# Low halves of split weights written one block later, splitting spread between matmul groups, and shared tiles in the hybrid attention units

## The chip, the cores and the metric

The kernel runs on one core of one Trainium2 chip. The metric is the device time of one execution in microseconds (us). The median of three runs is 2098.37 us. A core has TensorE (PE, with PEld for its weight loads), VectorE (DVE), ScalarE (ACT), GpSimd (POOL) and SyncE (SP, which here issues the loads of the weights). Each engine works through its own list of instructions in order and waits at semaphores for the others.

## The reference, cut to what matters

256 tokens of width 1024 pass two blocks of (feed-forward, attention, feed-forward), then a block with a hybrid attention (8 heads over a block of the sequence, 8 heads over the 64 keys that an indexer's top-k selects) and a mixture that picks experts by top-16 searches (PEER). All is float32.

```python
for i in range(2):
    kv = mem_n @ mem_w_kv[i]
    x = x + 0.5 * swiglu(rmsnorm(x, norm_g[i, 0]), ffn_w_up[i, 0], ffn_w_down[i, 0])
    h = rmsnorm(x, norm_g[i, 1])
    mix = pool_layer(h, ...) if i == 0 else diff_layer(h, ...)   # in-projection, attention, out-projection
    x = x + mix
    x = x + 0.5 * swiglu(rmsnorm(x, norm_g[i, 2]), ffn_w_up[i, 1], ffn_w_down[i, 1])
x = rmsnorm(x, final_norm_g)
mod = silu(c) @ w_ada + b_ada                                    # six rows: shifts, scales, gates
h = modulate(rms_norm(x, norm_attn), sh1, sc1)
x = x + g1 * hybrid_mixer(h, w_in, w_out, rel_bias)
h = modulate(rms_norm(x, norm_ffn), sh2, sc2)
x = x + g2 * peer_ffn(h, peer_wq, peer_subkeys, peer_u, peer_v)
return rms_norm(x, norm_final)
```

In the hybrid mixer each chunk of 128 queries does `score = einsum(wi, relu(qi @ k_idx))`, `top_k(score, 64)`, and a softmax over the selected keys; the other eight heads do a causal softmax with a position bias.

## The kernel before

Every float32 product is made of three matmuls. A factor is split into a high part that TensorE takes as it is and a low part, the rest: a block of weights `raw` [128 x 1024] is loaded by SP, ScalarE copies it to `whi` (L144), VectorE subtracts to `wlo` (L145), and `mm3` (L184 to L186) does high x high, the two mixed products, and no more. Activations are split the same way into `hT_hi` and `hT_lo` (L192 to L201).

The weights form one stream, `items`, in the order of use. `split_one` handles the next item of the stream: it emits `whi` and `wlo` (or, for an item with a `call`, a piece of the modulation row, two VectorE steps `acc` in `ada_piece`, L463 and L465). `nextw` gives out the next block and first splits as many blocks as `cfg["ahead"]` says, four, beyond it; `fetch(4)` asks for four blocks, enough for a projection of 512 columns. So when a group of matmuls is fetched, the splits of the next four blocks are written in one piece into the lists of ScalarE and VectorE. `load_to` issues the loads five blocks ahead.

`proj_cols` makes a projection in four quanta of 24 matmuls (8 blocks of 128 rows, three products each); a block of weights holds two of the eight, so the fourth block is first used by the 19th matmul and its low part by the 21st. Each quantum ends with `yield`, and the attention code interleaves it with steps of the softmax: the order of every engine's list is the order in which the Python code calls. After two quanta `evac` takes the result out; in the feed-forward layer (`ffn`) that is `silu` (L520 to L522) and `gate` (L532). `rows_mm` does the same with 12 matmuls of 512 columns, `out_proj_k` the out-projections, in which the last segments (`tail`) run row by row, with `update` (L1030, L1031), `stats` and `realT` (`ma`, `xg`, `hT_hi`; L343 to L355) of the next norm between them.

In the differential layer a unit's steps on VectorE are `e` (scores with bias, L850), `mx`, `nb`, the reciprocal `rc` and scalings (L866 to L872), `pt` (transposed probabilities, L884), `ov` (L911), then `cat_hi` and `cat_lo` (L198, L201), the operand of the out-projection.

The hybrid attention has eight units (`make(t, g)`: token half t, four heads g) of four steps: `s0` scores, bias, maximum and exponentials (one tile `e` for two heads, L1124 to L1142); `s1` reciprocals and four scalings on VectorE (L1148, L1152); `s2` eight or four transposes and the copy `pt` (L1164); `s3` the product with the values and the split of `yA` or `yB`. `pipeline` runs s1 of one unit, a quantum of the projections (`fill`), s0 of a later one, s3 and s2. `select` (L1090, L1091) runs ahead of all that: eight rounds of MAX and MATCH_REPLACE for each token half.

Of the kernel before, what the change touches and what calls it, by code (L numbers as in the profile page):

```python
# [60 lines left out]
def kernel(ctx: ExitStack, tc: tile.TileContext, A, LAY, stop=None):  # L61
# [41 lines left out]
    st = {"load": 0, "split": 0, "use": 0, "nsplit": 0, "raw": {}, "s": {}}  # L103
    deferred = []
    cfg = {"raw": 5, "ahead": 4}
# [288 lines left out]
    def out_proj_k(segs, update, nxt, tail=2, ahead=None):  # L394
# [12 lines left out]
        for gi in range(n - tail):  # L407
            gots[gi] = [fetch(1), fetch(1)]
            for t in range(NT):
                for h in range(2):  # L410
                    mm(t, h, [gi], gots)
                if t:
                    run_deferred()
                yield
# [5 lines left out]
        for t in range(NT):  # L420
            for h in range(2):
# [16 lines left out]
                if cut < n:  # L438
                    ahead.append(fetch(4))
                    cfg.update(was)  # L440
                yield
# [310 lines left out]
    n2 = Norm(A["norm_g"][0, 2])  # L752
    with pool("pl") as sp:
# [8 lines left out]
        def u_part(h):  # L762
            got = fetch(4)
            for t in range(NT):
                n1.before(t)
                p = pmm()
                rows_mm(p, hT, got[:4], t, 0, 512, 8)
                yield
                rows_mm(p, hT, got[4:], t, 0, 512, 8)
                ACT.activation(u[t][:, h * 512:(h + 1) * 512], p, AF.Copy, scale=n1.rstd[:, t:t + 1])  # L770
                if t:
                    run_deferred()
                yield
# [10 lines left out]
        def mixed():  # L784
# [4 lines left out]
            for ct in range(8):  # L789
# [6 lines left out]
                if ct % 2:  # L796
                    yield
# [8 lines left out]
        drain(fill)  # L806
    kv0.close()
# [13 lines left out]
    n5 = Norm(A["norm_g"][1, 2])  # L821
    with pool("df") as sp:
# [99 lines left out]
        def v_part(h):  # L922

            got = fetch(4)
            for t in range(NT):
                n4.before(t)
                p = pmm()
                rows_mm(p, hT, got[:4], t, 0, 512, 8)
                yield
                rows_mm(p, hT, got[4:], t, 0, 512, 8)  # L930
                ACT.activation(v[:, t, h * 512:(h + 1) * 512], p, AF.Copy, scale=n4.rstd[:, t:t + 1])
                if t:
                    run_deferred()
                yield
# [17 lines left out]
        drain(o)  # L952
    kv1.close()
# [49 lines left out]

    gotv, got = m1.got
# [95 lines left out]
    def v_part():  # L1100
        got = fetch(4)
        for t in range(NT):
            p = pmm()
            rows_mm(p, hT, got[:4], t, 0, 512, 8)
            yield
            rows_mm(p, hT, got[4:], t, 0, 512, 8)
            ACT.activation(av[:, t, 512:], p, AF.Copy)
            if t:
                run_deferred()
            yield  # L1110

    def make(t, g):

        w = (t + 1) * P
        b = {}

        def s0():
            pj = []
            for j in range(2):
                p = psm().rearrange("p (i s) -> p i s", i=2)  # L1120
                r = slice(j * 64, (j + 1) * 64)
                for i in range(2):
                    ct = 2 * g + i
                    PE.matmul(p[:, i, :w], aq[r, ct, t * P:(t + 1) * P], ak[r, ct, :w], start=True, stop=True)  # L1124
                pj.append(p)
            b["e"], b["s"] = [], []
            for j in range(2):
                bias = strip[:, 4 * g + j:4 * g + j + 3:2, S - w:]
                e = sp.tile([P, 2, S], F32, name="e", tag="e", bufs=6)
                V.scalar_tensor_tensor(e[:, :, :w], pj[j][:, :, :w], 0.125, bias, op0=OP.mult, op1=OP.add)  # L1130
                b["e"].append(e)
            if g >= 2:
                for j in range(2):
                    e = b["e"][j][:, :, :w]
                    V.tensor_tensor(e, e, M[:, t, None, :w].to_broadcast([P, 2, w]), op=OP.add)
            for j in range(2):
                e = b["e"][j]
                mx, nb, sm = (small([P, 2], x, bufs=6) for x in ("mx", "nb", "sum"))
                V.tensor_reduce(mx, e[:, :, :w], axis=AX.X, op=OP.max)
                V.tensor_scalar(nb, mx, -1.0, None, op0=OP.mult)  # L1140
                for i in range(2):
                    ACT.activation(e[:, i, :w], e[:, i, :w], AF.Exp, bias=nb[:, i:i + 1], accum_out=sm[:, i:i + 1])  # L1142
                b["s"].append(sm)

        def s1():
            rcs = [small([P, 2], "rc", bufs=6) for _ in range(2)]
            for j in range(2):
                V.reciprocal(rcs[j], b["s"][j])  # L1148
            for j in range(2):
                for i in range(2):  # L1150
                    e = b["e"][j][:, i, :w]
                    V.tensor_scalar(e, e, rcs[j][:, i:i + 1], None, op0=OP.mult)  # L1152

        def s2():
            n = 2 * (t + 1)
            b["p"] = []
            for j in range(2):
                p = ptr()
                for i in range(2):
                    for m in range(t + 1):  # L1160
                        c = i * (t + 1) + m
                        tr(p[:, c * P:(c + 1) * P], b["e"][j][:, i, m * P:(m + 1) * P])
                pt = sp.tile([P, 4, P], F32, name="pt", tag="pt", bufs=4)
                V.tensor_copy(pt[:, :n, :], p[:, :n * P].rearrange("p (m t) -> p m t", t=P))  # L1164
                b["p"].append(pt)

        def s3():
            p = psm()
            for i in range(2):
                for j in range(2):  # L1170
                    h = 4 * g + 2 * i + j
                    for m in range(t + 1):
                        PE.matmul(p[j * 64:(j + 1) * 64, i * P:(i + 1) * P], av[:, m, h * 64:(h + 1) * 64],
                                  b["p"][j][:, i * (t + 1) + m, :], start=m == 0, stop=m == t)
# [6 lines left out]
    for i, _ in enumerate(itertools.chain(proj_cols(hT, 4, 4, col_evac(aq, 0)), proj_cols(hT, 4, 4, col_evac(ak, 0)))):  # L1181
# [5 lines left out]
        else:  # L1187
            step(*se)
    drain(*se)
# [6 lines left out]
    for n, _ in zip(counts, pipeline(units, [(1, 2), (None, 0), (3, 3), (2, 2), (0, 0)])):  # L1196
        for _ in range(n):
            step(fill)
    drain(fill)
# [3 lines left out]

    got = m2.got
# [91 lines left out]
    q1st.close()  # L1296
    wstack.close()
# [337 lines left out]
```

## Time and profile before

| | before |
|---|---|
| median of 3 runs | 2098.37 us (2098.26 to 2100.83) |
| the profiled execution | 2098.71 us, its span 2096.9 us |
| mean granted clock of TensorE | 0.987 |
| TensorE busy | 2033.5 us (97%), 13678 matmuls |
| VectorE busy | 1458.4 us (70%) |
| ScalarE busy | 985.5 us (47%) |
| moved by DMA | 416.93 MB, 199 GB/s in the mean |

The stages in the profile: key and value projections of the memory until 62 us, feed-forward 62 to 255, pool layer to 350, feed-forward to 545 and to 735, differential layer to 893, feed-forward to 1086, hybrid attention to 1246, the query projection and top-16 to 1320, then the routing and the experts to 2097. A granted clock of 1.00 is 2.4 GHz; the other level is 1.2 GHz, and a window's figure is the mean over it.

### The profile page before, as it was taken

The page shows a single profiled execution, that of the slowest core. Times are in us where ns is not written, and L with a number is a line of the kernel's source. Part 1 is how long each engine was busy: PE and PEld are TensorE (multiplying, and loading weights), DVE is VectorE, ACT ScalarE, POOL GpSimd, SP SyncE. Part 2 cuts the span into 40 slices and gives each one's busy share as a digit, 9 for nine tenths or more (in the row PEclk, how much of TensorE's full clock was granted, in tenths as well). Part 3 has the DMA queues.
Part 4 walks back from the last instruction along what each step waited for, and adds up shares of the span by engine and source line. Part 5 has one row for each costly group of instructions (what it writes and reads, how often), then busy time and mean ns, then how long its engine had stood idle before and what let it go on. Part 6 is the DMA issues. An engine that isn't in the chain of part 4 may idle for free. (4 is left out here: it accounts for less than half of the span.)

```text
span 2096.9 us, 34488 instructions
## 1 busy us (share of the span) xinstructions
PE 2033.5 (97%) x13678; PEld 1832.0 (87%) x13678; DVE 1458.4 (70%) x2330; ACT 985.5 (47%) x1508; POOL 39.0 (2%) x74
## 2 busy tenths in 40 slices
PE   8999999999999998899989899999999999999998
PEld 7999888998999797799878779999998888888886
DVE  6677566776677568756658688889976666666666
ACT  6444454444444445354444344455554444444444
POOL 2000000000000000000000000000000000000000
PEclk9999999999999999999999899999999999999999
DMA  7667535676576552355545333556676776777764
GB/s 274 217 236 266 188 134 205 227 250 233 185 248 244 187 195 101 120 191 198 206 124 180 104 98 134 175 178 213 245 252 209 226 231 207 225 243 225 225 211 140
DMA packets 142379, 416.93 MB, mean 199 GB/s; under 512 B 12469, under 2 KB 47429, under 8 KB 140041
## 3 DMA queue, kind: packets, MB, share of 16 engines
q1 hardware_dynamic: 102672, 372.04, 52.4%
q10 hardware_dynamic: 37976, 36.91, 5.5%
q0 software_dynamic: 1568, 5.77, 0.9%
q8 instruction: 107, 1.75, 0.3%
q14 instruction: 56, 0.45, 0.1%
HBM read 396.82 MB, written 17.86 MB: 198 GB/s over the span
## 5 line engine op out<-in xcount | busy, mean ns | idle before, releaser
L145 DVE TENSOR_TENSOR wlo<-raw,whi 128x1024 fp32r<-128x1024 f32 (+1 forms) x654 | 780.6, 1222 | 329.8 <-ACT whi L144 329.5
L144 ACT ACTIVATE whi<-raw 128x1024 fp32r<-128x1024 f32 (+1 forms) x654 | 663.0, 1048 | 147.6 <-PE mm L186 85.4
L184 PE MATMUL mm<-hT_hi,whi 128*128 128x256 f32 x1680 | 479.9, 286 | 0.0
L185 PE MATMUL mm<-hT_lo,whi 128*128 128x256 f32 x1680 | 473.1, 282 | 0.0
L186 PE MATMUL mm<-hT_hi,wlo 128*128 128x256 f32 x1680 | 472.9, 281 | 0.0
L184 PEld LDWEIGHTS mm<-hT_hi,whi 128*128 128x128 f32 x1680 | 319.0, 190 | 6.5 <-issue 6.1
L185 PEld LDWEIGHTS mm<-hT_lo,whi 128*128 128x128 f32 x1680 | 318.9, 190 | 2.0 <-issue 1.9
L186 PEld LDWEIGHTS mm<-hT_hi,wlo 128*128 128x128 f32 x1680 | 318.7, 190 | 0.0
L184 PE MATMUL sm<-hT_hi,whi 128*128 128x256 f32 (+1 forms) x1048 | 299.5, 286 | 5.4 <-DVE hT_hi L192 2.2
L186 PE MATMUL sm<-hT_hi,wlo 128*128 128x256 f32 (+1 forms) x1048 | 296.5, 283 | 4.4 <-DVE wlo L145 4.4
L185 PE MATMUL sm<-hT_lo,whi 128*128 128x256 f32 (+1 forms) x1048 | 296.1, 283 | 0.4 <-DVE hT_lo L195 0.4
L184 PEld LDWEIGHTS sm<-hT_hi,whi 128*128 128x128 f32 (+1 forms) x1048 | 199.2, 190 | 8.7 <-DVE hT_hi L192 2.6
L184 PE MATMUL mm<-whi,wh 128*128 128x512 f32 x512 | 204.1, 399 | 2.1 <-ACT wh L194 2.1
L186 PEld LDWEIGHTS sm<-hT_hi,wlo 128*128 128x128 f32 (+1 forms) x1048 | 199.2, 190 | 4.8 <-DVE wlo L145 4.8
L186 PE MATMUL mm<-whi,wl 128*128 128x512 f32 x512 | 202.2, 395 | 0.0
L185 PEld LDWEIGHTS sm<-hT_lo,whi 128*128 128x128 f32 (+1 forms) x1048 | 199.3, 190 | 2.8 <-DVE hT_lo L195 0.6
L185 PE MATMUL mm<-wlo,wh 128*128 128x512 f32 x512 | 201.5, 394 | 0.0
L194 ACT ACTIVATE wh<-wf 128x256 fp32r<-128x256 f32 x128 | 53.5, 418 | 215.6 <-DVE wf L1484 215.6
L184 PE MATMUL mm<-whi,gT_hi 128*128 128x512 f32 x352 | 140.0, 398 | 0.0
L186 PE MATMUL mm<-whi,gT_lo 128*128 128x512 f32 x352 | 139.5, 396 | 0.0
L185 PE MATMUL mm<-wlo,gT_hi 128*128 128x512 f32 x352 | 138.6, 394 | 0.0
L1316 ACT ACTIVATE act<-sm 128x256 f32<-128x256 f32 x128 | 49.1, 384 | 166.3 <-PE sm L186 166.3
(308 smaller groups left out, 2615.9 us busy)
## 6 DMA issues: line engine op xcount, KB each, us to landing
raw<-in_ffn_up_dram SPq DMA_DIRECT2D x176, 512.0 KB, 5.2
raw<-in_peer_u_dram SPq DMA_DIRECT2D x128, 512.0 KB, 3.7
raw<-in_peer_v_dram SPq DMA_DIRECT2D x128, 512.0 KB, 3.8
raw<-in_ffn_dn_dram SPq DMA_DIRECT2D x88, 512.0 KB, 5.2
raw<-in_w_ada_dram SPq DMA_DIRECT2D x48, 512.0 KB, 5.0
gall<-stage ACTq DMA_DIRECT2D x16, 1024.0 KB, 4.6
G<-gall ACTq DMA_DIRECT2D x16, 1024.0 KB, 7.2
raw<-in_diff_w_in_dram SPq DMA_DIRECT2D x28, 512.0 KB, 5.5
```

The costliest lines, as they stand in the source:

```text
L144: ACT.activation(hi[:, :n], r[:, :n], AF.Copy)
L145: V.tensor_tensor(lo[:, :n], r[:, :n], hi[:, :n].bitcast(F32), op=OP.subtract)
L184: PE.matmul(out, a[0], b[0], start=start, stop=False)
L185: PE.matmul(out, a[0], b[1], start=False, stop=False)
L186: PE.matmul(out, a[1], b[0], start=False, stop=stop)
L194: ACT.activation(hi, src, AF.Copy)
L1316: ACT.activation(act[n], p, AF.Gelu)
```

## The change

The low half of a block is no longer emitted with its high half: `split_one` puts it on a list (`st["low"]`), and `low_one` emits it when a second one is pending, when the item is a `call`, or when `nextw` gives the block out. In the pool, differential and hybrid layers `cfg["spread"]` is set: `nextw` splits nothing ahead, and `ahead_one`, called after each quantum, splits one block if fewer than four are ahead. In the hybrid units the four heads of the first token half share one tile `e` and one maximum, the maximum is negated in its own instruction, one reciprocal serves four heads, and two of the four scalings are ScalarE's. The later steps of the second half's selection run between the steps of the first units.

```diff
+    def low_one():
+
+        j, r, p_ = st["low"].pop(0)
+        c = st["s"][j]
+        nk, w = items[j][1:3]
+        lo = p_.tile([P, CH], F32R, name="wlo", tag="wlo", bufs=4)
+        V.tensor_tensor(lo[:, :nk * w], r[:, :nk * w], c.hi.rearrange("p k w -> p (k w)").bitcast(F32), op=OP.subtract)
+        c.lo = lo[:, :nk * w].rearrange("p (k w) -> p k w", w=w)
+
     def split_one():
+
         j = st["split"]
-        load_to(j + cfg["raw"])
+        load_to(j + cfg["raw"] - len(st["low"]))
...
             hi = p_.tile([P, CH], F32R, name="whi", tag="whi", bufs=4)
-            lo = p_.tile([P, CH], F32R, name="wlo", tag="wlo", bufs=4)
             ACT.activation(hi[:, :n], r[:, :n], AF.Copy)
-            V.tensor_tensor(lo[:, :n], r[:, :n], hi[:, :n].bitcast(F32), op=OP.subtract)
-            st["s"][j] = Split(hi[:, :n].rearrange("p (k w) -> p k w", w=w), lo[:, :n].rearrange("p (k w) -> p k w", w=w))
+            st["s"][j] = Split(hi[:, :n].rearrange("p (k w) -> p k w", w=w), None)
+            st["low"].append((j, r, p_))
         st["split"] += 1
-        load_to(j + 1 + cfg["raw"])
+        while len(st["low"]) > 1 or st["low"] and call is not None:
+            low_one()
+        load_to(j + 1 + cfg["raw"] - len(st["low"]))
...
-        while k < len(items) and ahead < cfg["ahead"]:
+        while k < len(items) and ahead < cfg["ahead"] and not cfg["spread"]:
             ahead += items[k][3] is None
             k += 1
         while st["split"] < k:
             split_one()
+        while st["s"][j].lo is None:
+            low_one()
...
+    def ahead_one():
+
+        if cfg["spread"] and st["split"] < min(st["use"] + 4, len(items)):
+            split_one()
...
                 if j:
+                    ahead_one()
                     yield
                 proj_col(act, got, c0 + j, p[:, j * S:(j + 1) * S])
             evac(c0, m, p[:, :m * S].rearrange("p (j t) -> p j t", t=S))
+            ahead_one()
             yield
...
+            mx, sm = (small([P, 4], x, bufs=6) for x in ("mx4", "sum4"))
...
+            for k, e in enumerate(b["e"]):
+                c = k * heads
+                V.tensor_reduce(mx[:, c:c + heads], e, axis=AX.X, op=OP.max, negate=True)
+                for i in range(heads):
+                    ACT.activation(e[:, i], e[:, i], AF.Exp, bias=mx[:, c + i:c + i + 1], accum_out=sm[:, c + i:c + i + 1])
 
         def s1():
...
+            rc = small([P, 4], "rc4", bufs=6)
+            V.reciprocal(rc, b["s"])
+            for c in range(4):
+                e = b["e"][c // heads][:, c % heads]
+                if c < 2:
+                    V.tensor_scalar(e, e, rc[:, c:c + 1], None, op0=OP.mult)
+                else:
+                    ACT.activation(e, e, AF.Copy, scale=rc[:, c:c + 1])
...
-            step(*se)
-    drain(*se)
+            step(*(se if i == 1 else se[1:] if i == 7 else se[:1]))
...
+        if 1 <= i <= 4:
+            step(se[1])
+        elif i == 5:
+            drain(*se)
     drain(fill)
...
+    cfg["spread"] = False
     got = m2.got
```

TensorE's list is the same before and after, names aside; VectorE's and ScalarE's lists move. Three places follow. In the changed kernel L137 is `wlo`, L153 `whi`.

VectorE in the differential layer, where a unit's heads are put into `cat`, before:

```order
L872 SCALAR_TENSOR_TENSOR e<-e,rc 128x128 x2
L249 TENSOR_SCALAR ms<-oss 128x4
L145 TENSOR_TENSOR wlo<-raw,whi 128x1024 x4
L198 TENSOR_SCALAR cat_hi<-tr,sng 128x4x128
L201 SCALAR_TENSOR_TENSOR cat_lo<-tr,sng,cat_hi 128x4x128
```

and with the change:

```order
L901 SCALAR_TENSOR_TENSOR e<-e,rc 128x128 x2
L269 TENSOR_SCALAR ms<-oss 128x4
L137 TENSOR_TENSOR wlo<-raw,whi 128x1024 x2
L216 TENSOR_SCALAR cat_hi<-tr,sng 128x4x128
L219 SCALAR_TENSOR_TENSOR cat_lo<-tr,sng,cat_hi 128x4x128
```

Two of the four `wlo` have moved ahead, between the steps of the units before; the rest of the order is the same.

VectorE where the hybrid layer's out-projection ends and the modulated norm of the next part begins (`ma`, `xg`, `hT_hi`), before:

```order
L145 TENSOR_TENSOR wlo<-raw,whi 128x1024 x4
L1030 TENSOR_TENSOR xg<-mm,grow 128x512
L1031 TENSOR_TENSOR x_65<-x_65,xg 128x512
L192 CAST hT_hi<-sm 128x2x128
L195 TENSOR_TENSOR hT_lo<-sm,hT_hi 128x2x128
L1030 TENSOR_TENSOR xg<-mm,grow 128x512
L1031 TENSOR_TENSOR x_65<-x_65,xg 128x512
L320 SCALAR_TENSOR_TENSOR s_12355<-ssm 128x1
L337 TENSOR_SCALAR hh_12326<-x_65,r_12356 128x512
L1030 TENSOR_TENSOR xg<-mm,grow 128x512
L1031 TENSOR_TENSOR x_66<-x_66,xg 128x512
L343 SCALAR_TENSOR_TENSOR ma<-mod,cols 128x8
```

and with the change (the rows from `s` on):

```order
L340 SCALAR_TENSOR_TENSOR s_12243<-ssm 128x1
L357 TENSOR_SCALAR hh_12214<-x_65,r_12244 128x512
L1063 TENSOR_TENSOR xg<-mm,grow 128x512
L1064 TENSOR_TENSOR x_66<-x_66,xg 128x512
L137 TENSOR_TENSOR wlo<-raw,whi 128x1024 x4
L363 SCALAR_TENSOR_TENSOR ma<-mod,cols 128x8
L375 TENSOR_SCALAR xg<-tr,ma,mod 128x128 x4
L210 CAST hT_hi<-xg 128x4x128
```

The four `wlo` of the query weights stood ahead of the first update and stand now directly ahead of `ma`; on ScalarE the four `whi` have moved to between the last `junk` and its half of `xg`.

VectorE in the first feed-forward stage, at a gate that two `acc` follow (numbers tell the buffers apart), before:

```order
L507 TENSOR_TENSOR gT_lo_698<-gate_1335,gT_hi_697 128x512
L532 TENSOR_TENSOR gate_1469<-mm_1420,silu_1338 128x512
L465 SCALAR_TENSOR_TENSOR acc_1216<-raw_1343,cols_79,acc_1216 128x512 x2
L145 TENSOR_TENSOR wlo_1478<-raw_1347,whi_1477 128x1024
L145 TENSOR_TENSOR wlo_1484<-raw_1353,whi_1483 128x1024
```

and with the change:

```order
L530 TENSOR_TENSOR gT_lo_694<-gate_1331,gT_hi_693 128x512
L555 TENSOR_TENSOR gate_1465<-mm_1416,silu_1334 128x512
L488 SCALAR_TENSOR_TENSOR acc_1212<-raw_1345,cols_79,acc_1212 128x512 x2
L137 TENSOR_TENSOR wlo_1471<-raw_1339,whi_1357 128x1024
L137 TENSOR_TENSOR wlo_1481<-raw_1347,whi_1477 128x1024
```

The first `wlo` behind the `acc` is now the one of a block whose `whi` was written before (whi_1357), and TensorE's 21st matmul of the group that runs at that time reads it:

```order
L204 MATMUL mm_1501<-hT_hi_67,wlo_1359 128x256
L202 MATMUL mm_1501<-hT_hi_67,whi_1357 128x256
L203 MATMUL mm_1501<-hT_lo_68,whi_1357 128x256
L204 MATMUL mm_1501<-hT_hi_67,wlo_1471 128x256
L202 MATMUL mm_1501<-hT_hi_67,whi_1357 128x256
L203 MATMUL mm_1501<-hT_lo_68,whi_1357 128x256
```

In the list of before the low part for this matmul stood ahead of the `gate`. The same order, `gate`, two `acc`, `wlo`, stands at nine places of the first three feed-forward stages.

## Rows read from the trace of the kernel before

**Rows 1.** The page's busy times: us (share of the span) x instructions, by engine.

```profile
PE 2033.5 (97%) x13678; PEld 1832.0 (87%) x13678; DVE 1458.4 (70%) x2330; ACT 985.5 (47%) x1508; POOL 39.0 (2%) x74
```

**Rows 2.** Windows: span, busy (count) of PE, PEld, DVE, ACT, POOL; clock, DMA share, GB/s.

```profile
62.00:255.00 193.00, 193.00 (x1330) 178.32 (x1329) 135.27 (x162) 86.42 (x105) 1.75 (x4) 1.00 0.65 224
255.00:350.00 95.00, 92.62 (x512) 79.13 (x511) 59.87 (x93) 48.23 (x76) 3.07 (x4) 1.00 0.47 160
...
735.00:893.00 158.00, 144.04 (x942) 127.65 (x941) 112.98 (x240) 73.32 (x177) 4.62 (x5) 0.97 0.40 137
...
1086.00:1246.00 160.00, 142.02 (x893) 121.44 (x892) 121.99 (x280) 70.20 (x151) 6.21 (x8) 0.90 0.40 132
1246.00:1320.00 74.00, 67.82 (x463) 61.86 (x464) 64.79 (x282) 34.35 (x51) 2.47 (x3) 0.98 0.37 127
...
1145.00:1225.00 80.00, 70.05 (x429) 58.27 (x428) 59.13 (x149) 34.74 (x88) 0.00 (x0) 0.87 0.29 95
```

**Rows 3.** The page's costliest groups: busy us, mean ns | idle before, releaser.

```profile
L145 DVE TENSOR_TENSOR wlo<-raw,whi 128x1024 fp32r<-128x1024 f32 (+1 forms) x654 | 780.6, 1222 | 329.8 <-ACT whi L144 329.5
L144 ACT ACTIVATE whi<-raw 128x1024 fp32r<-128x1024 f32 (+1 forms) x654 | 663.0, 1048 | 147.6 <-PE mm L186 85.4
```

**Rows 4.** Waits of PE, 815 to 880 us: total us, times, longest.

```profile
PE tr L243 <- DVE cat_lo L201: 5.1, 2, 4.3
PE tr L243 <- DVE rc L867: 4.6, 1, 4.6
PE tr L243 <- DVE xscale L561: 2.8, 1, 2.8
PE tr L243 <- DVE rc L571: 1.3, 1, 1.3
```

**Rows 5.** Windows of 5 us in that stretch, columns as in rows 2.

```profile
820.00:825.00 5.00, 2.31 (x11) 2.34 (x12) 4.93 (x10) 0.30 (x1) 0.00 (x0) 0.74 0.86 309
...
865.00:870.00 5.00, 2.88 (x21) 2.26 (x20) 4.79 (x11) 0.00 (x0) 0.00 (x0) 1.00 0.58 210
```

**Rows 6.** Timeline, 816 to 823 us: start, length, instruction [idle before].

```profile
816.47 4.63 DVE L145 TENSOR_TENSOR wlo<-raw,whi 128x1024 fp32r<-128x1024 f32 x4 [0.78 <-ACT whi L144]
```

**Rows 7.** Waits of PE in the hybrid units, 1145 to 1225 us.

```profile
PE tr L243 <- DVE e L1152: 3.8, 1, 3.8
PE sm L1124 <- DVE e L1130: 2.4, 1, 2.4
PE sm L1124 <- DVE yA_lo L195: 2.0, 1, 2.0
PE sm L1124 <- DVE hT_lo L195: 1.8, 1, 1.8
```

**Rows 8.** Groups by form, 1145 to 1225 us: busy us, mean ns | idle before.

```profile
L1142 ACT ACTIVATE e<-e,nb 128x256 f32<-128x256 f32 x16 | 7.9, 497 | 23.9 <-DVE nb L1140 23.9
...
L1152 DVE TENSOR_SCALAR e<-e,rc 128x256 f32<-128x256 f32 x12 | 3.4, 349 | 0.0
```

**Rows 9.** Timeline of DVE, ACT and PE, 1226 to 1253 us.

```profile
1232.63 4.62 DVE L145 TENSOR_TENSOR wlo<-raw,whi 128x1024 fp32r<-128x1024 f32 x4
...
1244.44 1.37 DVE L355 TENSOR_SCALAR xg<-tr,ma,mod 128x128 f32<-128x128 f32 x4
...
1244.34 0.63 ACT L253 ACTIVATE junk<-x 128x512 bf16<-128x512 f32 x1 [1.18 <-DVE ma L343]
...
1246.32 0.50 PE L184 MATMUL mm<-whi,hT_hi 128*128 128x512 f32 x1 [0.78 <-DVE hT_hi L192]
```

**Rows 10.** Timeline of DVE and PE, 126 to 134 us.

```profile
129.51 0.69 DVE L532 TENSOR_TENSOR gate<-mm,silu 128x512 f32<-128x512 f32 x1 [0.25 <-PE mm L186]
130.12 1.53 DVE L465 SCALAR_TENSOR_TENSOR acc<-raw,cols,acc 128x512 f32<-128x512 f32 x2
...
129.31 0.28 PE L184 MATMUL mm<-hT_hi,whi 128*128 128x256 f32 x1
...
131.65 0.28 PE L186 MATMUL mm<-hT_hi,wlo 128*128 128x256 f32 x1
```

More of the change, by code (lines that the diff above doesn't have):

```diff
@@ L102 @@
     items = []
-    st = {"load": 0, "split": 0, "use": 0, "nsplit": 0, "raw": {}, "s": {}}
+    st = {"load": 0, "split": 0, "use": 0, "nsplit": 0, "raw": {}, "s": {}, "low": []}
     deferred = []
-    cfg = {"raw": 5, "ahead": 4}
+    cfg = {"raw": 5, "ahead": 4, "spread": False}
     CH = 1024
@@ L413, in out_proj_k @@
                     run_deferred()
+                ahead_one()
                 yield
@@ L440, in out_proj_k @@
                     cfg.update(was)
+                if not nxt.deep:
+                    ahead_one()
                 yield
@@ L752 @@
     n2 = Norm(A["norm_g"][0, 2])
+    cfg["spread"] = True
     with pool("pl") as sp:
@@ L772, in u_part @@
                     run_deferred()
+                ahead_one()
                 yield
@@ L796, in mixed @@
                 if ct % 2:
+                    ahead_one()
                     yield
@@ L821 @@
     n5 = Norm(A["norm_g"][1, 2])
+    cfg["spread"] = True
     with pool("df") as sp:
@@ L933, in v_part @@
                     run_deferred()
+                ahead_one()
                 yield
@@ L952 @@
         drain(o)
+    cfg["spread"] = False
     kv1.close()
@@ L1001 @@
         return dump(xt)
+    cfg["spread"] = True
     gotv, got = m1.got
@@ L1109, in v_part @@
                 run_deferred()
+            ahead_one()
             yield
@@ L1115, in make @@
         b = {}
+        parts = 2 if t else 1
+        heads = 4 // parts
         def s0():
-            pj = []
+            ps_ = [psm().rearrange("p (i s) -> p i s", i=2) for _ in range(2)]
             for j in range(2):
-                p = psm().rearrange("p (i s) -> p i s", i=2)
                 r = slice(j * 64, (j + 1) * 64)
                 for i in range(2):
-                    ct = 2 * g + i
-                    PE.matmul(p[:, i, :w], aq[r, ct, t * P:(t + 1) * P], ak[r, ct, :w], start=True, stop=True)
-                pj.append(p)
@@ L1136, in s0 @@
[L1136 to L1143, printed above, removed]
-        def s1():
[L1146 to L1152, printed above, removed]
+                    PE.matmul(ps_[j][:, i, :w], aq[r, 2 * g + i, t * P:(t + 1) * P], ak[r, 2 * g + i, :w], start=True, stop=True)
@@ new lines, in s0 @@
+            mx, sm = (small([P, 4], x, bufs=6) for x in ("mx4", "sum4"))
+            b["e"], b["s"] = [], sm
+            for j, p in enumerate(ps_):
+                if t or j == 0:
+                    b["e"].append(sp.tile([P, 2, S], F32, name="e", tag="e", bufs=6).rearrange("p i (a s) -> p (i a) s", s=w))
+                V.scalar_tensor_tensor(b["e"][j] if t else b["e"][0][:, j:j + 3:2], p[:, :, :w], 0.125,
+                                       strip[:, 4 * g + j:4 * g + j + 3:2, S - w:], op0=OP.mult, op1=OP.add)
@@ L1154, in s2 @@
         def s2():
-            n = 2 * (t + 1)
             b["p"] = []
-            for j in range(2):
+            for e in b["e"]:
                 p = ptr()
[L1159 to L1162, printed above, removed]
+                for c in range(4):
+                    i, m = divmod(c, t + 1)
+                    tr(p[:, c * P:(c + 1) * P], e[:, i, m * P:(m + 1) * P])
@@ L1171, in s3 @@
                     h = 4 * g + 2 * i + j
+                    pt, c = (b["p"][j], 2 * i) if t else (b["p"][0], 2 * i + j)
                     for m in range(t + 1):
                         PE.matmul(p[j * 64:(j + 1) * 64, i * P:(i + 1) * P], av[:, m, h * 64:(h + 1) * 64],
-                                  b["p"][j][:, i * (t + 1) + m, :], start=m == 0, stop=m == t)
+                                  pt[:, c + m, :], start=m == 0, stop=m == t)
             y, c = (yA, 2 * g) if g < 2 else (yB, 2 * g - 4)
@@ L1195 @@
     counts = [1, 0] + [1] * 7 + [0, 2, 0, 1, 0, 2, 0, 1, 0, 2, 1, 0, 0]
-    for n, _ in zip(counts, pipeline(units, [(1, 2), (None, 0), (3, 3), (2, 2), (0, 0)])):
+    for i, (n, _) in enumerate(zip(counts, pipeline(units, [(1, 2), (None, 0), (3, 3), (2, 2), (0, 0)]))):
         for _ in range(n):
             step(fill)
+        if 1 <= i <= 4:
+            step(se[1])
+        elif i == 5:
+            drain(*se)
     drain(fill)
@@ L1201 @@
         return dump(xt)
+    cfg["spread"] = False
     got = m2.got
@@ L1296 @@
     q1st.close()
+    while st["low"]:
+        low_one()
     wstack.close()
```

16 lines of the change are left out of this document (6 added, 10 removed).

## The prediction

> **What bounds the kernel now.** I read the page's busy times first: TensorE works 97% of the span [rows 1], so about 63 us of it are left to win, and nothing that makes VectorE or ScalarE faster counts by itself. Then the windows by stage [rows 2]: in the feed-forward stage from 62 to 255 us TensorE is busy 193.00 of 193 us, while the differential-attention stage (735 to 893 us) leaves it 14.0 us idle and the hybrid stage (1086 to 1246 us) 18.0 us. The same rows give the granted clock: 0.97 and 0.90 in these two, 1.00 in the feed-forward stage. That is 0.03 x 158 = 4.7 us and, over the 142 us that TensorE works, 0.10 x 142 = 14.2 us more. So the two attention stages hold some 32 us of idle time and 19 us of slow clock, and the feed-forward stages hold nothing but risk: whatever makes TensorE wait there is lost in full.
>
> The waits say what the idle time is. In the differential layer there are five of them [rows 4]: 4.3 and 0.8 us before transposes for `cat_lo`, 4.6 us for a reciprocal, 2.8 us and 1.3 us. The timeline shows what stands ahead: four `wlo` in a row, 4.63 us of VectorE, just before `cat_hi` and `cat_lo` [rows 6]. One `wlo` is 1.22 us, one `whi` on ScalarE 1.05 us [rows 3]. The hybrid units have four waits of the same kind, 3.8, 2.4, 2.0 and 1.8 us [rows 7], together 10.0 us.
>
> The clock follows the longer waits. In the 5 us slice with the first wait it is 0.74, and in the slice with the waits of 1.3 and 0.8 us it is 1.00 [rows 5]. So a wait of some 2 us or more costs TensorE's clock as well (from 2.4 to 1.2 GHz for a part of the next slices), one of 1.3 us did not.
>
> **Differential layer.** The change leaves the number of `wlo` as it is and spreads them: two stand ahead of the first `cat_hi` where four did, one ahead of `ov` where two did. The first wait loses two `wlo`, 2.3 us, and the work ahead of them moves little because as many have to be done until there (eight before, seven now): I take 4.3 to 1.5. The second wait, behind two `whi` and two `wlo`, vanishes, since one of each is done earlier: 4.6 to 0. The third loses one `wlo` and part of the wait for its `whi`: 2.8 to 1.0. The last two go from 2.1 to 0.8 together. Sum 10.5 us. The clock's 4.7 us go with the three long waits; I take 3.5. Term: **-14.0** (bounds -10 and -15.2, all idle time named and all clock).
>
> **Pool layer.** Idle there is 2.4 us [rows 2], and the bursts are of the same kind: **-1.0** (0 to -2).
>
> **Group boundaries in these layers.** Spreading has a price. The low part of a group's fourth block is now written only when the group is fetched, behind the evacuation of the group before (about a VectorE step of 0.69 us as the gate's [rows 10]) and after another `wlo`: 0.69 + 2 x 1.2 = 3.1 us after the boundary. It is wanted by the 21st matmul of the group, 2.34 us after the first [rows 10]. That is up to 0.7 us at six boundaries, less at some: **+2.8** (0 to +4.5).
>
> **Hybrid units and selection.** Of the 10.0 us of waits the two behind four `wlo` (3.8 and 2.0 us) lose their cause, and the fourth its two. What stays: in the first unit the selection's later steps now stand between the unit's own steps on VectorE, so the wait of 2.4 us only shrinks to about 2; and two of four scalings go to ScalarE, where they stand behind the four exponentials of the next unit, 4 x 0.50 us [rows 8]. I take 2 us for that, at one unit. So 10.0 to 4.0. The stretch from 1145 to 1225 us has a clock of 0.87 [rows 2], 0.13 x 70.05 = 9.1 us lost, 2.3 us for each of the four waits; two of them go: 4.6. With 0.4 us for small waits of the stage: **-11.0** (bounds 0 and -19, all of both). The step on VectorE costs 0.35 us [rows 8] and the same size on ScalarE 0.50, taken from the exponential. The Trainium skill ("ScalarE: Activation LUTs", section "Rules for kernel authors") says to multiply on VectorE and not on ScalarE; the rows agree in direction, 0.50 against 0.35. By the rule alone the 16 scalings moved would cost ScalarE 8.0 us where VectorE gives up 5.6.
>
> **Feed-forward stages: a new wait.** Here the low part of the fourth block is late too, and nine times something stands ahead of it that did not: the two `acc` steps of a modulation weight. Now `gate` starts 0.20 us after the group, ends after 0.69 us, the two `acc` take 1.53 us from 130.12 on, and the `wlo` 1.22 us: it ends at 130.12 + 1.53 + 1.22 = 132.87. The group's 21st matmul, the first that reads it, starts at 131.65 in the profile of before [rows 10]. The wait is 1.2 us, nine times: **+10.8**, in stages where TensorE is busy all the time and has nothing to win it back with. Bounds: 0, if VectorE reaches the gate or the `acc` earlier than the order says, and 9 x 2.3 more if every such wait pulls the clock down. Where no `acc` stands there, `gate` and `wlo` end at 131.34, 0.3 us ahead of the reader: nothing, but with little cover. If that cover is gone, each tenth of a microsecond counts at every such group.
>
> The Trainium skill ("TensorE: Matmul & The Clock Gate", section "A second HAM failure mode: psum-queue depth-cycling") tells of a kernel in which frequent short idles of TensorE made its clock swing between the two levels. The row with waits of 1.3 and 0.8 us at a clock of 1.00 [rows 5] speaks against it at this length; I use the row.
>
> **Query projection: a moved burst.** While `spread` is set, the fetch does not split four blocks ahead. Before, the four `wlo` of the query weights ran at 1232.63 us under the out projection [rows 9]. Now they are fetched between it and the modulated norm: four `whi` on ScalarE behind `junk` (which ended at 1244.97), four `wlo` on VectorE, and behind them `ma`, `xg` and `hT_hi`, for which the query matmul waits; from the start of `xg` to that matmul it was 1246.32 - 1244.44 = 1.9 us [rows 9]. From 1244.97: 1.05 for the first `whi`, 4.6 for four `wlo`, 2.0 for the rest, that is 1252.6, against 1246.32 before: 6.3 us. VectorE comes 4.6 us earlier to the updates ahead, which can bring `junk` forward by 1.7 us, to where the out projection's matmuls end: 4.6. A stall of this length lowers the clock: up to 1.7 more. I take **+6.0** (bounds 4.6 and 8; 0 if the chain behind it has slack, for which I see no row: the top-16 part behind it keeps VectorE busy, 64.8 of 74 us [rows 2]).
>
> **Sum.** -14.0 - 1.0 + 2.8 - 11.0 + 10.8 + 6.0 = -6.4. The profiled execution took 2098.71 us (span 2096.9), so 2092.3; the median of the runs is 2098.37, 0.34 less, so I forecast **2092.0 us**.
>
> **The rivals.**
> *The new waits don't come.* If the order at the nine places is met with time to spare, the feed-forward term is 0: 2092.0 - 10.8 = 2081.2 us, and without the query projection's 6.0 too 2075. For it: a margin of VectorE could be hidden in the pipeline of matmul issue. Against: the order has the `acc` ahead, and their times are in the rows.
> *Slower: ScalarE's scalings become the chain.* In each of eight units the transposes wait for two steps that stand behind four exponentials, and sometimes one or two `whi`, on ScalarE: 4 x 0.50 + 1.05 + 2 x 0.50 = 4.05 us, where VectorE had four steps of 0.35 = 1.4 us. If 1.4 us of the difference shows in all eight units, the -11.0 is gone: 2103.0 us. The point from which it decides is about 0.8 us a unit (8 x 0.8 = 6.4, the whole sum). For it: waits of 2 us come with a lower clock. Against: the units are pipelined, two or three steps of TensorE lie between.
> *Slower: the clock falls at the nine waits.* 9 x 2.3 = 20.7 us on top: 2112.7 us. Against it stands the slice at 1.00 [rows 5]. The Trainium skill's rule on short idles, above, would give this one.
> *Waits only move.* VectorE does the same work in total; if the differential layer's waits reappear at the group boundaries, its 14 us shrink to about 8: 2098 us.
>
> **How the numbers follow.** A measurement of this kernel tells 0.2%, 4.2 us, from no change. Chances: the forecast 0.50, its own range 2087 to 2097 from the bounds of its terms; new waits absent 0.16; ScalarE's chain 0.16; waits only move 0.12; the clock 0.06. Faster by over 0.2% (under 2094.2): 0.36 of the forecast and 0.16 = 0.52. Within: 0.14 and 0.12 = 0.26. Slower: 0.22. The range reaches to the first rival's 2081 and to the second's 2103, with a microsecond: 2080 to 2104.
>
> **What would show it.** In the profile after: the waits for `cat_lo` and `rc` in the differential layer under 2 us, the clock there at 0.99; nine waits of TensorE for `wlo` of some 1.2 us between 62 and 735 us, at a clock of 1.00; one wait of 5 to 6 us for `hT_hi` near 1245 us; in the units a wait or two of transposes for ScalarE. I am wrong if the feed-forward stages show no wait for `wlo` or many, or if the units wait at every scaling.

## The result, and the profile after

The changed kernel takes 2122.34 us (median of 4 runs, 2120.13 to 2122.96) against 2098.32 us before: a ratio of 1.0111, interval [1.0093, 1.0128]. The profiled execution has a span of 2121.2 us. The forecast was 2092.0 us, faster, with a range of 2080 to 2104; the kernel is 24 us slower.

First the windows of the changed kernel by stage, columns as in [rows 2]: the start, the first feed-forward stage, the differential layer, the hybrid layer, the query projection with the top-16. The stages lie later than before.

```profile
0.00:40.00 40.00, 26.41 (x117) 22.70 (x118) 21.91 (x33) 23.10 (x37) 11.29 (x37) 0.91 0.75 262
72.00:265.00 193.00, 189.97 (x1315) 175.32 (x1314) 132.11 (x156) 84.81 (x101) 0.56 (x1) 1.00 0.65 224
...
759.00:917.00 158.00, 144.93 (x947) 126.66 (x945) 111.47 (x239) 75.27 (x179) 7.28 (x5) 0.99 0.39 134
...
1110.00:1257.00 147.00, 132.48 (x894) 112.33 (x892) 109.91 (x221) 72.20 (x162) 6.21 (x8) 0.98 0.40 130
1257.00:1343.00 86.00, 73.00 (x478) 66.96 (x479) 72.89 (x299) 39.59 (x58) 2.47 (x3) 0.92 0.39 129
```

The hybrid layer has become 13 us shorter and its clock went from 0.90 to 0.98; the differential layer's clock from 0.97 to 0.99, but its idle time of 13.1 us is nearly that of before (14.0). In the hybrid layer the idle time fell only from 18.0 to 14.5 us; TensorE's busy time for as many matmuls fell from 142.0 to 132.5, so most of the gain there is clock. The feed-forward stage, which had no idle time, has 3.0 us. The query stage is 12 us longer, at a clock of 0.92. Then the waits of TensorE over the whole execution, the six longest groups (total, times, longest):

```profile
PE mm L204 <- DVE wlo L137: 27.9, 24, 4.5
PE mm L202 <- DVE hT_hi L210: 10.8, 2, 7.1
PE tr L263 <- DMA mem<-in_mem_dram: 7.5, 2, 4.8
PE mm L203 <- DVE wlo L137: 7.3, 3, 3.2
PE sm L204 <- DVE wlo L137: 4.5, 5, 1.8
PE tr L263 <- DVE e L901: 2.3, 1, 2.3
```

Waits for a `wlo` add up to 39.7 us in 32 places (before: 4.4 us in two); the waits of [rows 4] and [rows 7] for `cat_lo`, `rc`, `e` and `yA_lo` are mostly gone. The time went from one kind of wait to the other.

TensorE's list is the same in both kernels, so the start of the n-th matmul can be taken from both traces and subtracted. How this lag grows from stage to stage says where the time went. The table has it for the whole change and for three of the experiments below: the lag alone, the whole change without the lag, and the lag in the attention layers alone (us; the stretches are numbers of matmuls, with the time before at which they begin).

| stretch | before, us | whole change | lag alone | no lag, rest | lag in attention |
|---|---|---|---|---|---|
| start, 0 to 200 | 5 | +9.5 | +8.2 | +0.2 | 0.0 |
| feed-forward 0, to 1700 | 43 | +4.0 | +4.1 | +0.6 | 0.0 |
| pool layer, to 2150 | 264 | -0.1 | -0.9 | +4.5 | -0.8 |
| head of feed-forward 1, to 2200 | 346 | +3.9 | 0.0 | +2.3 | 0.0 |
| feed-forward 1 and 2, to 4800 | 357 | +6.5 | +7.0 | -1.2 | -0.1 |
| differential layer, to 5700 | 737 | -1.9 | -1.8 | +8.4 | -1.3 |
| feed-forward 3, to 6990 | 887 | +2.3 | 0.0 | +3.8 | 0.0 |
| hybrid layer, to 7900 | 1078 | -12.6 | -10.0 | +5.7 | -9.4 |
| query, top-16, to 8400 | 1241 | +9.6 | +5.1 | +5.6 | +1.9 |
| rest, to 13677 | 1322 | +3.0 | 0.0 | -0.6 | -0.8 |

The column of the whole change adds up to 24.2 us. Each column is one execution: in stretches where a kernel's lists are those of before, the lag still moves by up to 1.4 us, in the last stretch by up to 2.5 us, so single small entries say little.

Two of the new waits are where the prediction put them. The timeline of the changed kernel at the gate of [rows 10]: the two `acc` end at 142.7, the `wlo` behind them one step later, and the 21st matmul has waited 1.02 us. There are nine such waits, 1.0 us each; the clock is 1.00 at all of them.

```profile
140.60 0.69 DVE L555 TENSOR_TENSOR gate<-mm,silu 128x512 f32<-128x512 f32 x1 [1.99 <-PE mm L204]
141.20 1.53 DVE L488 SCALAR_TENSOR_TENSOR acc<-raw,cols,acc 128x512 f32<-128x512 f32 x2
142.65 3.49 DVE L137 TENSOR_TENSOR wlo<-raw,whi 128x1024 fp32r<-128x1024 f32 x3
...
143.92 0.39 PE L204 MATMUL mm<-hT_hi,wlo 128*128 128x256 f32 x1 [1.02 <-DVE wlo L137]
```

And the query projection, where [rows 9] showed 0.78 us: four `whi` on ScalarE, four `wlo` on VectorE, then `ma`, `xg`, `hT_hi`, and a wait of 7.13 us.

```profile
1255.87 3.88 ACT L153 ACTIVATE whi<-raw 128x1024 fp32r<-128x1024 f32 x4
...
1256.94 4.63 DVE L137 TENSOR_TENSOR wlo<-raw,whi 128x1024 fp32r<-128x1024 f32 x4 [1.80 <-ACT whi L153]
...
1263.73 0.77 PE L202 MATMUL mm<-whi,hT_hi 128*128 128x512 f32 x1 [7.13 <-DVE hT_hi L210]
```

The third place is not as forecast: a group's fourth low half in the differential layer. The timeline shows it behind the steps of a whole unit and behind a wait for ScalarE (`ms` for `junk`), not behind one evacuation. TensorE waits 4.5 us in the middle of the group.

```profile
845.72 0.61 DVE L901 SCALAR_TENSOR_TENSOR e<-e,rc 128x128 f32<-128x128 f32 x2
847.17 0.17 DVE L269 TENSOR_SCALAR ms<-oss 128x4 f32<-128x4 f32 x1 [0.84 <-ACT junk L273]
847.25 2.35 DVE L137 TENSOR_TENSOR wlo<-raw,whi 128x1024 fp32r<-128x1024 f32 x2
...
848.52 0.49 PE L204 MATMUL mm<-hT_hi,wlo 128*128 128x256 f32 x1 [4.51 <-DVE wlo L137]
```

### The profile page after: what moved, and what is told of

The parts are those of the page before. It is cut to its first block, busy times and chain, and to the rows that moved or that the text cites. A ratio compares the mean times of both kernels' runs of the same rounds, so it can differ in the third digit from the quotient of the medians.

```text
span 2121.2 us, 34196 instructions
## 1 busy us (share of the span) xinstructions
PE 2037.5 (96%) x13678; PEld 1832.2 (86%) x13678; DVE 1435.8 (68%) x2280; ACT 988.1 (47%) x1524; POOL 44.6 (2%) x74
## 4 chain that ended last, share of the span: by engine, by line
PE 84%; DVE 11%; ACT 3%; issue 2%; DMA 1%; ACTq 0%; POOL 0%; POOLq 0%; DVEq 0%; SPq 0%
PE mm L204 21%; PE mm L202 21%; PE mm L203 21%; PE sm L204 5%; PE sm L202 5%; PE sm L203 5%; DVE wlo L137 4%; PE mm L1472 2%; PE tr L263 1%; ACT junk L273 1%; DVE i L1266 1%; ACT whi L153 1%; DVE v L1264 0%; DMA mem<-in_mem_dram 0%; DVE e L879 0%
## 5 line engine op out<-in xcount | busy, mean ns | idle before, releaser
L137 DVE TENSOR_TENSOR wlo<-raw,whi 128x1024 fp32r<-128x1024 f32 (+1 forms) x654 | 779.1, 1218 | 133.5 <-ACT whi L153 132.5
L153 ACT ACTIVATE whi<-raw 128x1024 fp32r<-128x1024 f32 (+1 forms) x654 | 669.4, 1049 | 184.4 <-DMA raw<-in_ffn_up_dram 67.9
L213 DVE TENSOR_TENSOR wl<-wf,wh 128x256 fp32r<-128x256 f32 x128 | 54.5, 425 | 200.0 <-ACT wh L212 200.0
```

The lines of the kernel that those rows point to most:

```text
L137: V.tensor_tensor(lo[:, :nk * w], r[:, :nk * w], c.hi.rearrange("p k w -> p (k w)").bitcast(F32), op=OP.subtract)
L213: V.tensor_tensor(lo, src, hi.bitcast(F32), op=OP.subtract)
```

## The experiments

Three parts can be taken apart: the late low halves ("the lag"), the spread splitting, and the hybrid units with their selection. My theory after the result (A) was that the lag costs the time; the rival (B) that the spreading does.

### The lag taken out, and the lag alone

```diff
-        while len(st["low"]) > 1 or st["low"] and call is not None:
+        while st["low"]:
```

> The changed kernel with every wlo emitted right behind its whi again; spread splitting, hybrid units and selection stay. Theory A (the late low halves cost the time: raw buffers are held longer, so the loads at the start and at the heads of the feed-forward stages run dry, and nine gates wait): the start's 9.9 us, the nine gates' 9.2 us and some 5 us at the stage heads go, 2085 to 2098 us. Rival B (spreading in the attention layers costs it, the low halves are harmless): no feed-forward stage changes, 2115 to 2123 us.

2131.11 us (2127.88 to 2132.27), ratio 1.0153 [1.0131, 1.0174], outside both forecasts. The whole change without its lag is slower still. The start and the gates are as before, as A says, but all three attention layers are now slower than before (column "no lag, rest" of the table).

The lag alone is the kernel before with `low_one`, the list and the loop above, and nothing else of the change.

> The kernel before with the late low halves alone (no spread, units and selection as before). Theory A: the start +10 us, nine gates +9, the head of a feed-forward stage +2 to +4, so 2117 to 2124 us, as slow as the whole change. Rival B: 2096 to 2102 us.

2110.4 us (2106.92 to 2115.87), ratio 1.0059 [1.0041, 1.0078]. It loses at the start, at the gates and in the query and top-16 stage what the whole change loses there (less 4.5 us in the latter), and it wins 10.0 us in the hybrid layer without any new units and without spread. So A and B both fall as they stood: the lag costs outside the attention layers and is what wins inside them; the spread costs inside when it comes without the lag. Call that theory C. With the lag the spread costs little inside: over the differential layer the whole change gains 1.9 us and the lag alone 1.8.

Why spreading without the lag costs shows in VectorE's waits, first of that kernel (differential, then hybrid layer), then of the whole change, then of the kernel before:

```profile
DVE wlo L137 <- ACT whi L153: 27.1, 17, 4.0
...
DVE wlo L137 <- ACT whi L153: 41.0, 21, 3.2
```

```profile
DVE wlo L137 <- ACT whi L153: 5.5, 2, 2.9
...
DVE wlo L137 <- ACT whi L153: 12.6, 11, 1.8
```

```profile
DVE wlo L145 <- ACT whi L144: 11.2, 5, 5.9
...
DVE wlo L145 <- ACT whi L144: 10.3, 7, 2.6
```

A single `whi` stands between exponentials in ScalarE's list, and a `wlo` right behind it in VectorE's list holds up all of the softmax until ScalarE comes to it: 41.0 us of waits against 10.3 before. TensorE then waits for the softmax's steps in turn, in the hybrid layer of the kernel without the lag:

```profile
PE tr L263 <- DVE e L1183: 7.7, 2, 7.2
PE sm L1160 <- DVE yA_lo L213: 6.5, 4, 2.2
```

With the lag a `wlo` mostly finds its `whi` done: 12.6 us of waits are left there, none above 1.8.

### The lag where it wins

```diff
-        while len(st["low"]) > 1 or st["low"] and call is not None:
+        while len(st["low"]) > (1 if cfg["spread"] else 0) or st["low"] and call is not None:
```

> The changed kernel with late low halves only while spread is set (pool, differential and hybrid layers). Theory A: start and gates are as before, 2095 to 2101 us; what it lies above the run with low halves at once is the price of the lag at the group boundaries of the attention layers, 3 to 8 us. Rival: the lag there is worth what it was made for, and this run is the faster of the two by over 3 us.

2101.78 us (2098.95 to 2104.09), ratio 1.0015 [1.0005, 1.0025]. Start, gates and top-16 are back; what is left above before is the query projection (6.8 us), the heads of the feed-forward stages (2.6 and 3.9 us) and the boundaries in the differential layer. The rival on the lag inside the layers is right: without it there, the same kernel takes 2131.

The next is the kernel before with the lag in the pool, differential and hybrid layers alone (a flag `lag` set and cleared where the change sets and clears `spread`).

> The kernel before with late low halves in the pool, differential and hybrid layers alone (no spread, units and selection as before). Theory C, from the run with the lag alone: what wins in the attention layers is the lag (there -0.9 in the pool layer, -1.8 in the differential, -10 in the hybrid layer) and what loses lies outside (start, gates, top-16, routing): 2084 to 2090 us. Rival (spread and the new units win, the lag only costs): 2096 us or more.

2087.66 us (2086.91 to 2090.83), ratio 0.9953 [0.9936, 0.997]: 11 us under before, the lowest median of the study, as theory C says. Here is its timeline (and TensorE's wait) at the longest wait of [rows 7], 3.8 us before:

```profile
1162.99 1.22 DVE L137 TENSOR_TENSOR wlo<-raw,whi 128x1024 fp32r<-128x1024 f32 x1
1165.38 3.50 DVE L137 TENSOR_TENSOR wlo<-raw,whi 128x1024 fp32r<-128x1024 f32 x3 [1.17 <-ACT whi L153]
...
1169.33 0.92 PE L256 MATMUL tr<-ident,e 128*128 128x128 f32 x4 [0.93 <-DVE e L1170]
```

The pending low half of the block before runs while ScalarE is still at the exponentials, so VectorE waits 1.17 us for the first `whi` of the burst, and three low halves are left behind that wait, not four. To test that, the same kernel with the pending low half emitted at the end of each quantum of matmuls:

```diff
+    def quantum():
+        if cfg["lag"] and st["low"]:
+            low_one()
...
+                quantum()
                 yield
```

> As the kernel with the lag in the attention layers alone (2087.7 us), but the pending low half is emitted at the end of each quantum of matmuls, so that it never waits for the next fetch. If the wait of 3.9 us for a late low half in the differential layer goes and the hybrid layer keeps its 10 us: 2081 to 2086 us. If the gain in the hybrid layer hangs on the low half that starts the next burst (it needs no new high half), it is lost in part: 2089 to 2095 us.

2097.49 us (2093.18 to 2101.76), ratio 0.9991 [0.9979, 1.0003]: the gain is lost. Its timeline at the same place has four `wlo` after 2.30 us of waiting, and TensorE waits 3.87 us, as it did before (3.8 us [rows 7]):

```profile
1168.60 4.63 DVE L137 TENSOR_TENSOR wlo<-raw,whi 128x1024 fp32r<-128x1024 f32 x4 [2.30 <-ACT whi L153]
...
1173.68 1.12 PE L262 MATMUL tr<-ident,e 128*128 128x128 f32 x4 [3.87 <-DVE e L1185]
```

The late low half in the differential layer went too: up to matmul 5400 the lag of this run is 0.0 us, against +6.5 with the plain lag. But what the plain lag gives back behind that, 7.9 us, went with it.

With two low halves held back and one emitted per quantum:

```diff
-        while len(st["low"]) > (1 if cfg["lag"] else 0) or st["low"] and call is not None:
+        while len(st["low"]) > (2 if cfg["lag"] else 0) or st["low"] and call is not None:
```

> As the run before, with two low halves held back and one emitted at the end of each quantum, so that a burst on VectorE is two or three instead of four. If the length of the burst is what costs: 1 to 5 us under the run before. If late low halves at the group boundaries eat it: above it.

2089.04 us (2088.27 to 2090.75), ratio 0.9955 [0.9941, 0.9969]: 8 us under the run before, more than forecast, and level with the plain lag in the attention layers. At the same place VectorE again waits 2.30 us for the first `whi`, but three `wlo` follow and the fourth comes behind the scalings that TensorE waits for:

```profile
1160.39 3.50 DVE L137 TENSOR_TENSOR wlo<-raw,whi 128x1024 fp32r<-128x1024 f32 x3 [2.30 <-ACT whi L153]
...
1164.34 0.91 PE L262 MATMUL tr<-ident,e 128*128 128x128 f32 x4 [2.68 <-DVE e L1185]
```

So it is not needed that a burst begins with a low half whose high half is done. What the two good kernels share is that fewer low halves of the new burst, three and not four, stand between the wait for ScalarE and the steps that TensorE needs. How much of the 8 us comes from this place is not shown: TensorE's wait here is 2.68 us in the one and 0.93 in the other, and the two kernels are level.

### The hybrid units

The units and selection of the change, on the kernel with the lag in the attention layers, and by themselves (no lag, no spread).

> As the run before, with the changed hybrid units and selection too, still without spread. If the units add to the lag's gain: 2078 to 2086 us. If the lag had already taken the waits that they were made for: within 2 us of the run before.

2089.85 us (2088.25 to 2091.47), ratio 0.9958 [0.9941, 0.9975]: within 2.2 us of the run without them, they add nothing.

> The kernel before with the changed hybrid units and selection alone: no lag, no spread. If sharing tiles and moving two scalings to ScalarE is worth something by itself, 2090 to 2096 us; if ScalarE's scalings become the chain (the rival of the prediction), 2099 us or more with waits of transposes for ScalarE.

2099.96 us (2097.03 to 2102.51), ratio 1.0004 [0.9995, 1.0014]: no change. The time is that of the forecast's upper case, the cause is not: TensorE's long waits there are 3.7 us for VectorE's `e`, 3.0 for `yA_lo` and 2.1 for `hT_lo`, none of them for ScalarE. The scalings in the groups by line, ScalarE's and VectorE's (busy us, mean ns):

```profile
L1184 ACT ACTIVATE e<-e,rc 128x128 f32<-128x128 f32 (+1 forms) x16 | 6.3, 443 | 4.8 <-DVE rc L1178 4.8
...
L1182 DVE TENSOR_SCALAR e<-e,rc 128x128 f32<-128x128 f32 (+1 forms) x16 | 4.4, 317 | 0.3
```

A step that moved costs 443 ns on ScalarE against 317 for one that stayed. The sixteen that left VectorE relieve it by about as much as the sixteen that stayed cost, 4.4 us, and the time does not follow: the waits are still there. The Trainium skill ("ScalarE: Activation LUTs", section "Rules for kernel authors") prefers VectorE for a multiplication; the means agree in direction, and here it decides nothing. Each of the three waits stands behind a burst of low halves that begins with a wait of VectorE for ScalarE's `whi`:

```profile
1168.39 4.63 DVE L137 TENSOR_TENSOR wlo<-raw,whi 128x1024 fp32r<-128x1024 f32 x4 [2.50 <-ACT whi L153]
...
1191.29 4.63 DVE L137 TENSOR_TENSOR wlo<-raw,whi 128x1024 fp32r<-128x1024 f32 x4 [2.73 <-ACT whi L153]
...
1212.08 2.36 DVE L137 TENSOR_TENSOR wlo<-raw,whi 128x1024 fp32r<-128x1024 f32 x2 [2.96 <-ACT whi L153]
```

Before, VectorE waited 2.30, 0.96 and 1.89 us at these places: its waits there grew by 3.0 us, against the 4.4 us of scalings that it no longer has.

### The query projection

```diff
-        cfg.update(ahead=8 - 2 * tail)
+        cfg.update(ahead=8 - 2 * tail, spread=cfg["spread"] and not nxt.deep)
```

on the kernel with the lag in spread only:

> Lag only in the attention layers, spread there except in the tail of the hybrid out-projection, where four blocks are split ahead as before. Theory: the moved burst before the query projection costs about 7 us, so 2101.8 - 7 = 2093 to 2096 us, with the wait for hT_hi near 1245 us back under 1 us. Rival (the burst would have to stand somewhere else in that stretch and cost the same): 2100 us or more.

2096.92 us (2094.13 to 2100.72), ratio 0.9993 [0.9983, 1.0003], 4.9 us less than without the edit and a little above the forecast. In the traces the step in lag at the query projection falls from 6.8 to 0.7 us, and the longest wait for `hT_hi` there from 7.1 to 0.8 us. The moved burst is the cause.

### The gates and the start

On the whole change, a pending low half ahead of the two `acc`:

```diff
         if call is not None:
+            while st["low"]:
+                low_one()
             call(r[:, :n].rearrange("p (k w) -> p k w", w=w))
```

> The whole change, but a pending low half is emitted ahead of the two acc steps instead of behind them. If the nine waits of 1.0 us at the gates come from this order, they vanish and nothing else moves: 2122.3 - 9.4 = 2111 to 2115 us. If they have another cause (TensorE's readers, the loads), 2119 to 2123 us.

2113.23 us (2111.86 to 2114.73), ratio 1.007 [1.0052, 1.0088]: 9.1 us less, as forecast. The nine waits are gone; the waits for `wlo` fall from 24 to 15:

```profile
PE mm L206 <- DVE wlo L137: 18.3, 15, 3.9
```

At the start I had blamed the weights' buffers: a `raw` block is held until its low half is made, SP's next loads wait for it (39.6 us of waits in the first 40, against 22.5 before), and the loads run dry. One more buffer and one more load ahead for the first 90 items:

```diff
+    def more(n):
+        return n + 1 if n < 90 else n
...
+            if st["load"] < 90 and st["load"] % 6 == 5:
+                r = wpool3.tile([P, CH], F32, name="raw", tag="raw", bufs=1)
...
```

> The changed kernel with one more raw buffer, and one more load ahead, for the first 90 items of the stream (until late in the first feed-forward stage). If the start loses its 10 us because a raw buffer is held by the low half that comes late, the start is back within 3 us of before and the time is 2112 to 2116 us, with the nine waits of about 1 us at the gates still there. If it is VectorE's order that makes it late, the time stays at 2120 to 2123 us.

2121.62 us (2120.14 to 2124.39), ratio 1.0108 [1.0085, 1.013]: nothing. TensorE's waits in the first 45 us are what they were in the change, 3.2 and 2.8 us for a `wlo`, so the buffers are not the cause:

```profile
PE tr L270 <- DMA mem<-in_mem_dram: 7.3, 2, 4.7
PE mm L210 <- DVE wlo L144: 3.2, 1, 3.2
PE mm L211 <- DVE wlo L144: 2.8, 1, 2.8
```

With the low halves of the first 16 blocks at once (the whole change otherwise):

```diff
-        while len(st["low"]) > 1 or st["low"] and call is not None:
+        while len(st["low"]) > (1 if j >= 16 else 0) or st["low"] and call is not None:
```

> The whole change, but the first 16 blocks (the key and value projections of the memory) have their low halves at once. If the 10 us at the start are VectorE's order there (the first low half stands behind the norm's steps, the eighth behind the next fetch), the start is as before: 2111 to 2114 us. If something later in the stream makes up for it, 2118 us or more.

2117.28 us (2112.29 to 2118.08), ratio 1.0088 [1.0071, 1.0106]: 5.1 us less, not 10: between the two cases of the forecast. The profiled execution is the one of 2112.29, and in it the waits for `wlo` at the start are 0.2 us and the lag after 200 matmuls is 0.2 us, against 9.5:

```profile
PE tr L263 <- DMA mem<-in_mem_dram: 7.2, 2, 4.7
PE tr L263 <- DVE hT_lo L213: 0.4, 1, 0.4
PE mm L203 <- DVE wlo L137: 0.2, 1, 0.2
```

So in this trace the place is right: VectorE's order at the start, where the first `wlo` stands behind the norm's steps (13.8 us instead of 8.9). Why the other three runs took 2117 us is open; no trace of them is shown here.

## Why the prediction was wrong

**The feed-forward gates**: right, place and order; 9.1 us instead of 10.8, since the waits are 1.0 and not 1.2 us. The rival that the clock falls there did not come: it is 1.00 at all nine. The Trainium skill ("TensorE: Matmul & The Clock Gate", section "A second HAM failure mode: psum-queue depth-cycling") speaks of frequent short idles that made the clock swing; nine of 1.0 us, some 36 us apart within a stage, did not do it.

**The query projection**: right. Forecast +6.0, bounds 4.6 and 8; the wait is 7.13 us where it was 0.78, and undoing it takes 6.1 us out of the trace (4.9 by the medians).

**The differential layer**: the waits between matmuls 5400 and 5700 give back 15.4 us, near the forecast of -14.0, but not by spreading alone, as I had it: the lag alone gives 8.1 there and the spread without the lag 2.3. The step that failed is the group boundaries: "behind the evacuation of the group before and after another `wlo`", +2.8 with a bound of +4.5. Up to matmul 5400 the layer loses 13.6 us. Of these 7.7 are waits for a late `wlo`, in eight places, 4.5 us the longest; 2.3 are a wait for the scaled `e`, which I did not have (the spread without the lag has four of that kind, 7.2 us in all); the rest, 3.6 us, is not split further, and the lower clock behind the long wait, 0.87 and then 0.79 in the two slices of 5 us from 845 us on, is part of it. I worked out one boundary between projections, where VectorE has little else, and took it for all; at the longest the late low half stands behind a unit's softmax steps, which wait for ScalarE in their turn.

**The hybrid layer**: -12.6 against a forecast of -11.0, right in size by luck and wrong in cause. I had the gain from spreading and from the units; by the trace the units alone give -1.5 (nothing in the medians), spreading without the lag, with the units, +5.7, and the lag alone -10.0. The parts are off as well: idle time gave 3.5 us and the clock most of the rest, where I had 6.0 and 4.6. The rival on ScalarE's scalings did not come. The pool layer gave 0.1 where I had 1.0.

**Everywhere else**: the step that failed and cost most is the sentence that where no `acc` stands ahead, the late low half costs nothing. I had worked it out for the feed-forward groups and let it stand for the whole kernel. The start (+9.5), where the groups follow each other while VectorE prepares a norm, and the top-16 and later stages (about 6.6 us of the last two rows of the table) were never gone through; the sum has nothing for them. Without the lag outside the attention layers the start is 0.0 and the two rows are +1.9 and -0.8. The heads of feed-forward 1 and 3 (+3.9 and +2.3) come with the spread: with the lag alone they are 0.0. At each TensorE has one wait, 2.0 us for a `wlo`; at the first, that is the first of five in a row behind the norm's steps, as at the query projection:

```profile
361.29 5.76 DVE L137 TENSOR_TENSOR wlo<-raw,whi 128x1024 fp32r<-128x1024 f32 x5
```

The rest of the 3.9 us there is the clock (0.70 from 362 to 367 us). ScalarE waits 4.1 us for loads behind that, for which TensorE does not wait. No run moved this burst alone.

Taken together: forecast -6.4, measured in the traces +24.2. The start, +9.5, the differential layer up to matmul 5400, 10.8 more than forecast, the heads, +6.2, and the top-16 and later, about +6.6, make up the difference of 30.6 us, with some 2.4 us the other way.

## What to carry to other kernels

When one engine's instruction needs another's result, it matters less how its instructions are spread than how long the in-order list stands still for the operand, and how much stands between that wait and the step that the bottleneck needs: one block of distance between producer and consumer took 9 to 10 us out of the hybrid layer, and spreading without that distance made VectorE wait four times as long there. The same distance is a loss wherever the consumer's consumer is near, so go through every stage that the shared code serves, the start too, before an edit in a helper is costed at nothing. Turned on where it wins and off elsewhere, it gave 2087.7 us, below both kernels.

## What the runs showed of the hardware

Waits of TensorE of 1.0 us left the granted clock at 1.00 in the feed-forward stages, which I had expected from [rows 5]. My line that a wait of some 2 us or more costs the clock fits the trace of before: during or just behind each of its nine waits of 2.0 to 4.6 us, those of the start aside, the clock falls to the lower level. It does not fit the changed kernel. The windows there, columns as in [rows 2], hold a wait of 2.0 us at the head of a feed-forward stage, one of 2.3 us in the differential layer and one of 2.0 us at the head of another feed-forward stage; only the first was followed by the lower clock. The third, 2.0 us again, did lower it in the kernel with the lag in spread only (0.66 from 899 to 904 us). What decides it is open.

```profile
362.00:367.00 5.00, 4.44 (x15) 3.54 (x16) 5.00 (x5) 3.08 (x4) 1.44 (x2) 0.70 0.64 197
835.00:840.00 5.00, 4.28 (x24) 3.26 (x24) 4.90 (x17) 2.60 (x11) 1.04 (x1) 1.00 0.34 108
918.00:923.00 5.00, 4.33 (x21) 3.56 (x22) 5.00 (x5) 3.18 (x4) 1.77 (x3) 1.00 0.64 188
```

What I had not expected is how little a thinner list helps an engine that waits in order: VectorE had 16 scalings fewer in the hybrid units, and the kernel took 2099.96 us, the same as before within the interval. Three long waits of TensorE (3.7, 3.0 and 2.1 us) stood behind bursts for whose operands VectorE itself had waited 2.50, 2.73 and 2.96 us.
